# Hybrid encoder trunk: more seven-product tiles on the second feed-forward matrices, at other places

## The chip, the cores and the metric

The kernel runs on one core of a Trainium2 chip. The time is device microseconds of one launch. In the profile PE is TensorE (matmuls), PEld its weight loads, DVE the vector engine, ACT the scalar engine, SP the engine that issues most DMAs.

## The reference

Two layers on x of 256 tokens by 2048 features, everything in fp32: layer 0 is a 2-D neighbourhood attention (16 heads of 128), layer 1 a dilated windowed attention (three groups of eight heads). After each attention comes a feed-forward of width 8192, and at the end one more norm. What matters here is the feed-forward:

```python
def rms_norm(x, g):
    y = xf * lax.rsqrt(jnp.mean(xf * xf, axis=-1, keepdims=True) + EPS)
    return y * g

def sq_relu_mlp(h, w1, w2):
    return jnp.square(jax.nn.relu(h @ w1)) @ w2
...
for i in range(DEPTH):
    ...
    x = x + sq_relu_mlp(rms_norm(x, g), w1, w2)      # w1: 2048 x 8192, w2: 8192 x 2048
return rms_norm(x, final_norm)
```

Each feed-forward streams two matrices of 64 MB once through the core.

## The kernel before

**Products.** All of x stays in SBUF. Every fp32 operand is cut into a high and a low part in the matmul's format (`wh` and `wl` for weights): ACT rounds the high part, DVE subtracts it to get the low part. A product is three matmuls of 512 columns, high-high, high-low and low-high (`three`, lines 197 to 201).

**Steps.** The work is a list of 400 steps, issued in order. While step i's matmuls run in four quarters, `prep` cuts the weights of step i + 2 (lines 147 to 187), `load` fetches those of step i + 5, and small tasks (transposes, softmax pieces, norms) are hung into quarters. Every engine works through its own instructions in that order. Three buffers hold raw weights, four each hold halves of `wh` and `wl`.

**Calls, tiles and places.** In the feed-forwards the steps come in calls of `gemm_pair`, eight steps each. A call multiplies all 256 tokens by 1024 columns of a matrix, over a depth of 2048. One step is one **tile**, 256 deep, numbered 0 to 7 by its depth; its **place** (also 0 to 7) is when in the call it runs. A tile is a 2 by 2 by 2 block product, and is done in one of two ways:

- kind `"s"`: eight block products, 24 matmuls. `prep` makes two halves of `wh` and `wl`.
- kind `"x"`: seven block products (Winograd's form of Strassen's scheme), 21 matmuls. `prep_x` also adds blocks of the weights on DVE (`sums`, three instructions, and the block of `w` that is replaced), ACT rounds three sums (`hs`) and DVE makes their low parts (`ls`). The left operand needs sums too: `sums_and_parts` takes four 128-column blocks and makes the sums S1 to S3 and the parts, S1 standing in place of the block A21. With `keep` it leaves A21 and makes S1 as a fourth sum, so that the tile can be used either way.

The seven-product tiles of a call share four more PSUM banks ("1", "5", "6", "7"). In the place after the last of them `begin` combines these banks into the SBUF tile `C`. The last step's banks are added to `C` (`last_sum`) or the result goes to x (`early` adds `C` to x, `put` adds the call's other four banks).

**Groups.** A feed-forward (`ffn`) has four groups g of 2048 hidden features. A group has four calls: two on the first matrix (`cp` 0 and 1), each giving 1024 hidden features, then two on the second matrix over the depth of these 2048. After a call on the first matrix, `hidden` has ACT apply scale, relu and square to `C` (two instructions a quarter, during place 0 of the next call), PE transposes them at place 1, and four tiles of `hT` are made: a plain tile by one copy and one subtraction; a seven-product one by a copy to `raw` and, some places later, `parts_of`, which calls `sums_and_parts`.

In an eight-place order below, s and x are the kinds at places 0 to 7.

| call | tiles of kind x | order |
|---|---|---|
| first matrix, first call, g = 0 | 2, 4, 6 | ssxsxsxs |
| first matrix, first call, g > 0 | 2, 5, 4, 6 | ssxxsxxs |
| first matrix, second call | 2, 4, 6 | ssxsxsxs |
| second matrix, both calls, g < 3 | 2, 3, 5 | ssxsxsxs |
| second matrix, first call, g = 3 | 3, 5 | sssxsxss |
| second matrix, second call, g = 3 | 3, 5 | ssssxxss, in the second feed-forward ssxsxsss |

Tile 5 of the norm's output is the kept one: eight products in some calls, seven in others. A group's `early` additions to x, 1024 columns and twice 512, hang in the call that follows. In the last call of a feed-forward the last two steps are parted (`split_end`), so that half of the result is ready earlier.

Of the kernel before, what the change touches and what calls it, by code (L numbers as in the profile page):

```python
# [14 lines left out]
P = 128  # L15
T = 256
# [32 lines left out]
def tile_encoder(ctx: ExitStack, tc: tile.TileContext, ins, out):  # L49
# [324 lines left out]
    class Norm:  # L374
# [60 lines left out]
        def rstd(self):  # L435
            self.root()
            self.inverse()
            r = self.r
            self.rw = small.tile([P, 2, P], F32, name="rw", tag="rw", bufs=1)
            nc.vector.tensor_copy(self.rw, r.unsqueeze(2).to_broadcast([P, 2, P]))  # L440
# [7 lines left out]
        def rows_out(self):  # L448
            self.bc = small.tile([P, T], F32, name="rbc", tag="rbc", bufs=1)
# [19 lines left out]

    def sums_and_parts(b, t, half, sums):  # L470

        hi, lo = (t[:, 2 * half:2 * half + 2, h, :].rearrange("p a (u t) -> p a u t", u=2) for h in range(2))
        whole = b[:, 3:7, :].rearrange("p (a u) t -> p a u t", u=2)
        keep = sums.shape[2] == 4

        def own():
            nc.scalar.copy(hi, whole)
            subtract(nc.vector, lo, whole, hi.bitcast(F32))

        if keep:  # L480
# [6 lines left out]
        for n, src in ((slice(0, 3), b[:, 0:3, :]), (slice(3, 4), b[:, 4:5, :]))[:1 + keep]:  # L487
# [3 lines left out]
        for n, src in ((slice(0, 3), b[:, 0:3, :]), (slice(3, 4), b[:, 4:5, :]))[:1 + keep]:  # L491
            subtract(nc.vector, sums[:, 1, n], src, sums[:, 0, n].bitcast(F32))
# [47 lines left out]
    def pending_norm(get, bc):  # L540

        def chunk_done(step, c, delay=0, late=0):
            i = steps.index(step)
            for half in range(2):
                at(i + 1 + delay, lambda half=half: get().transposes(c, half), lambda half=half: get().parts(c, half),
                   quarter=1 + half + late)
            if c == NB - 1:
                if not bc:
                    at(i + 4, None, lambda: get().root())
                    at(i + 5, None, lambda: get().inverse())  # L550
                else:
                    at(i, None, lambda: get().rstd())
                    at(i + 2, lambda: get().rows(), lambda: get().rows_out())
                if get().perm:
                    at(i + 3, lambda: get().cols(), lambda: get().cols_out())
        return chunk_done
# [143 lines left out]

    FF_PAIRS, FF_KEPT = (2, 4, 6), (5,)
# [5 lines left out]
    out_rows(ins["na_wo"], na_oT, 4, lambda: norms[1], begin_norm(1, False, FF_PAIRS, FF_KEPT),  # L707
             [(c, k) for c in range(3) for k in range(3)] + [(c, 3) for c in range(3)] + [(3, k) for k in range(4)], 2)


    def ffn(norm, w1, w2, next_norm, next_done):
        for g in range(4):
            last = g == 3
            pairs2 = (3, 5) if last else (2, 3, 5)
            hT, sums = [None] * 4, {}

            def hidden(made, q, cp, hT=hT, sums=sums, pairs2=pairs2, last=last):
                i = steps.index(made[-1]) + 1
# [13 lines left out]
                for r in range(4):  # L732
# [10 lines left out]
                    def post(r=r, held=held):  # L743
                        c, half, pair = 2 * cp + r // 2, r % 2, 4 * cp + r
                        if half == 0:
                            hT[c] = opool.tile([P, 4, 2, T], F32R, name="hT", tag="o")
                        if pair in pairs2:
                            raw = blocks()
                            nc.scalar.copy(raw[:, 3:7, :].rearrange("p (a u) t -> p a (u t)", u=2), held["t"])

                            def parts_of(c=c, half=half, raw=raw, pair=pair):
                                sums[pair] = part.pool.tile([P, 2, 3, P], F32R, name="hs", tag="hsum", bufs=3)
                                sums_and_parts(raw, hT[c], half, sums[pair])
                            steps[i + (3 if cp else 2 * r - 1)].after[1].append(parts_of)
                        else:
                            to = hT[c][:, 2 * half:2 * half + 2]
                            split(to[:, :, 0, :], to[:, :, 1, :], held["t"])
# [3 lines left out]
            for cp in range(2):  # L761
                more = g and not cp
                order = ff_order(FF_PAIRS + FF_KEPT, (0, 1, 2, 5, 3, 4, 6, 7)) if more else ff_order(FF_PAIRS)
                gemm_pair(w1, 2 * g + cp, norm.xT, norm.sums, order, lambda made, q, cp=cp: hidden(made, q, cp))
# [6 lines left out]
            def residual(made, q, cp, parted, last=last):  # L771
# [12 lines left out]
                if not parted:  # L784
                    i = steps.index(made[-1])
                    for n in range(2):
                        if last:
                            made[-1].after[n].append(lambda n=n: early(n))
                        else:
                            at_after(i + (4 + 2 * n, 3 + 3 * n)[cp], 1, lambda n=n: early(n))  # L790
                    for m, (tb, c) in enumerate(QUARTERS):
# [23 lines left out]
            for cp in range(2):  # L815
                parted = last and cp == 1
                order = range(8) if last else (0, 1, 2, 4, 3, 6, 5, 7)
                if parted:
                    order = ((0, 1, 2, 4, 3, 5, 6, 7), (0, 1, 3, 2, 5, 4, 6, 7))[next_done is None]
                gemm_pair(w2g, cp, hT, sums, ff_order(pairs2, order), lambda made, q, cp=cp, parted=parted: residual(made, q, cp, parted),  # L820
                          parted, parted and next_done is not None)

# [133 lines left out]
    for hh in range(2):  # L956
# [16 lines left out]
        for h in range(4):  # L973
# [4 lines left out]
    parts[len(steps) + 2] = "feed-forward"  # L978
    out_rows(ins["dil_wo"], dil_oT, 2, lambda: norms[3], begin_norm(3, False, FF_PAIRS, FF_KEPT),
             [(0, 0), (1, 0), (0, 1), (1, 1), (2, 0), (2, 1), (3, 0), (3, 1)])  # L980
# [106 lines left out]
    for c in range(NB):  # L1087
        steps[(0, 1, 2, 2)[c]].post.append(lambda c=c: n0.squares(c))
    steps[2].post.append(n0.rstd)
# [102 lines left out]
```

## Time and profile before

| | us |
|---|---|
| median of 3 runs (2255.87 to 2257.86) | 2256.42 |
| the profiled execution | 2253.24 |
| its span, first to last instruction | 2251.5 |
| PE busy, DVE busy, ACT busy | 2238.7, 1891.8, 1269.2 |
| first feed-forward, from its first tile to its last call's first tile | 397.81 to 1035.90 |
| second feed-forward, the same | 1560.24 to 2199.14 |

A timeline row gives the start, the length, the engine, the source line, what is written from what, how many instructions were merged and, in brackets, the idle time before them with what ended it. A row of windows gives the busy time of each engine within a stretch. A matmul's record is longer than the time from one matmul to the next, since they are pipelined, and back-to-back DVE records overlap by less than 0.1 us. Counts such as x64 are of instructions in the stretch asked for.

### The profile page before, as it was taken

To read this page: it belongs to the slowest core of one execution; us is meant where nothing else is said; L and a number is where in the kernel's file an instruction comes from. 1 tells how busy PE (TensorE), PEld (TensorE's weight loads), DVE (VectorE), ACT (ScalarE), POOL (GpSimd) and SP (SyncE) were. 2 spreads that over 40 slices of the span, in tenths; PEclk is the share of its full clock that TensorE was granted. 3 is DMA by queue.
4 is the path that set the end of the run, shared out by engine and by line. 5 is a ranking of instruction groups with operands and counts; after the bars stand their busy time and mean duration, and the time that the engine had idled before them with its cause. 6 is when DMAs were issued, how large, how long until landed. Compare 5 with 4: busy or idle time off the path is not lost.

```text
span 2251.5 us, 28385 instructions
## 1 busy us (share of the span) xinstructions
PE 2238.7 (99%) x10906; PEld 1883.4 (84%) x10906; DVE 1891.8 (84%) x2217; ACT 1269.2 (56%) x1582; POOL 0.7 (0%) x6
## 2 busy tenths in 40 slices
PE   9999999999999999999999999999999999999998
PEld 8888888888888888888888888888888888888886
DVE  6776666899999999989877667757999999999988
ACT  6555455665665565565444544456665665665664
POOL 0000000000000000000000000000000000000000
PEclk9999999999999999999999999999999999999999
DMA  7556554656656666665555445444666666666664
GB/s 256 177 186 192 177 180 165 203 187 209 202 188 207 200 192 206 196 190 190 209 180 186 170 169 183 172 169 151 208 201 197 199 205 192 200 204 192 204 218 136
DMA packets 110728, 430.33 MB, mean 191 GB/s; under 512 B 23872, under 2 KB 24448, under 8 KB 92160
## 3 DMA queue, kind: packets, MB, share of 16 engines
q1 hardware_dynamic: 109920, 426.82, 58.1%
q8 instruction: 85, 1.39, 0.2%
q10 hardware_dynamic: 672, 1.70, 0.2%
q14 instruction: 51, 0.42, 0.1%
HBM read 426.38 MB, written 2.10 MB: 190 GB/s over the span
## 4 chain that ended last, share of the span: by engine, by line
PE 98%; DVE 1%; ACT 1%; issue 0%; ACTq 0%; POOLq 0%; POOL 0%; DVEq 0%
PE banks L199 25%; PE banks L201 25%; PE banks L200 25%; PE banks L229 13%; PE banks L234 7%; PE banks L740 1%; PE banks L393 1%; PE banks L940 0%; PE banks L900 0%; PE banks L635 0%; PE banks L1072 0%; PE banks L918 0%; PE banks L920 0%; ACT wh L194 0%; DVE wl L195 0%
## 5 line engine op out<-in xcount | busy, mean ns | idle before, releaser
L195 DVE TENSOR_TENSOR wl<-w,wh 128x1024 fp32r<-128x1024 f32 (+1 forms) x802 | 963.1, 1217 | 235.0 <-ACT wh L194 148.3
L194 ACT CAST wh<-w 128x1024 fp32r<-128x1024 f32 (+1 forms) x802 | 824.6, 1048 | 457.0 <-PE banks L201 306.3
L199 PE MATMUL banks<-wh,xT 128*128 128x512 f32 x1074 | 423.3, 394 | 0.0
L200 PE MATMUL banks<-wl,xT 128*128 128x512 f32 x1074 | 418.7, 390 | 0.0
L201 PE MATMUL banks<-wh,xT 128*128 128x512 f32 x1074 | 418.5, 390 | 0.0
L199 PE MATMUL banks<-wh,hT 128*128 128x512 f32 x804 | 316.2, 393 | 0.0
L201 PE MATMUL banks<-wh,hT 128*128 128x512 f32 x804 | 313.2, 390 | 0.0
L200 PE MATMUL banks<-wl,hT 128*128 128x512 f32 x804 | 312.9, 389 | 0.0
L229 PE MATMUL banks<-xT,wh 128*128 128x512 f32 x1280 | 312.5, 392 | 0.0
L229 PEld LDWEIGHTS banks<-xT,wh 128*128 128x128 f32 x1280 | 233.4, 188 | 44.2 <-ACT wh L194 0.2
L180 ACT CAST hs<-sums 128x1536 fp32r<-128x1536 f32 x98 | 145.3, 1482 | 186.5 <-DVE sums L138 186.5
L201 PEld LDWEIGHTS banks<-wh,xT 128*128 128x128 f32 x1074 | 201.6, 188 | 42.2
L200 PEld LDWEIGHTS banks<-wl,xT 128*128 128x128 f32 x1074 | 201.9, 188 | 40.6 <-DVE wl L195 1.2
L199 PEld LDWEIGHTS banks<-wh,xT 128*128 128x128 f32 x1074 | 201.9, 188 | 39.7
L201 PEld LDWEIGHTS banks<-wh,hT 128*128 128x128 f32 x804 | 150.9, 188 | 31.6
L200 PEld LDWEIGHTS banks<-wl,hT 128*128 128x128 f32 x804 | 151.1, 188 | 30.3
L135 DVE TENSOR_TENSOR ls<-sums,hs 128x1536 fp32r<-128x1536 f32 x98 | 171.6, 1751 | 5.6 <-ACT hs L180 5.6
L199 PEld LDWEIGHTS banks<-wh,hT 128*128 128x128 f32 x804 | 151.0, 188 | 30.0
L234 PE MATMUL banks<-xT,wl 128*128 128x256 f32 x1280 | 172.7, 284 | 0.1
L234 PEld LDWEIGHTS banks<-xT,wl 128*128 128x128 f32 x1280 | 165.8, 191 | 6.6 <-DVE wl L195 0.6
L138 DVE TENSOR_TENSOR sums<-w 128x1024 f32<-128x1024 f32 x98 | 119.4, 1218 | 0.0
L199 PE MATMUL banks<-wh,oT 128*128 128x512 f32 x192 | 76.6, 399 | 0.0
(186 smaller groups left out, 2348.7 us busy)
## 6 DMA issues: line engine op xcount, KB each, us to landing
w<-in_ffn_w_dram SPq DMA_DIRECT2D x512, 512.0 KB, 4.7
w<-in_dil_wqkv_dram SPq DMA_DIRECT2D x72, 1024.0 KB, 4.8
w<-in_na_wqkv_dram SPq DMA_DIRECT2D x47, 1024.0 KB, 5.2
w<-in_na_wo_dram SPq DMA_DIRECT2D x16, 1024.0 KB, 4.8
w<-in_dil_wo_dram SPq DMA_DIRECT2D x8, 1024.0 KB, 4.7
bias<-in_rpb_dram SPq DMA_DIRECT2D x32, 96.0 KB, 10.0
out_dram<-x SPq DMA_DIRECT2D x8, 256.0 KB, 2.6
x<-in_x_dram SPq DMA_DIRECT2D x3, 512.0 KB, 9.0
```

The source lines that it names most:

```text
L135: engine.tensor_tensor(out=out, in0=a, in1=b, op=ALU.subtract)
L138: engine.tensor_tensor(out=out, in0=a, in1=b, op=ALU.add)
L180: nc.scalar.copy(s.hs, s.sums)
L194: nc.scalar.copy(dst_hi, src)
L195: nc.vector.tensor_tensor(out=dst_lo, in0=src, in1=dst_hi.bitcast(F32), op=ALU.subtract)
L199: nc.tensor.matmul(o, left[0], right[0], start=start, stop=False)
L200: nc.tensor.matmul(o, left[0], right[1], start=False, stop=False)
L201: nc.tensor.matmul(o, left[1], right[0], start=False, stop=stop)
L229: nc.tensor.matmul(acc[j // 2][:, j % 2, :], s.hi[a][:, j * P:(j + 1) * P], xT[k][:, a].rearrange("p h t -> p (h t)"), start=k == 0 and a ...
L234: nc.tensor.matmul(acc[j // 2][:, j % 2, :T], s.lo[a][:, j * P:(j + 1) * P], xT[k][:, a, 0, :], start=False, stop=k == nk - 1 and a == 3)
L393: nc.tensor.transpose(self.tp[:, a, tb * P:(tb + 1) * P], x[:, tb, kt * P:(kt + 1) * P], ident)
L740: nc.tensor.transpose(t[:, a, tb * P:(tb + 1) * P], q["C"][:, 2 * tb + f // 4, f % 4 * P:(f % 4 + 1) * P], ident)
```

## The change

The second matrices' tile 6 becomes a seven-product tile in the second call of groups 0 to 2. In the first call it still is an eight-product one, so it is prepared with `keep`, but without the fourth sum: `first_sum` replaces A21 by S1 in place, at place 2 of the second call, from the difference of the parts. In the last group tile 2 joins tiles 3 and 5 in both calls. Orders and places change with it:

| call | tiles of kind x | order |
|---|---|---|
| first matrix, first call | unchanged, but the kept tile of the second feed-forward is 3 instead of 5 | as before |
| first matrix, second call | 2, 4, 6 | sssxsxxs |
| second matrix, first call, g < 3 | 2, 3, 5 | sssxsxxs |
| second matrix, second call, g < 3 | 2, 3, 5, 6 | ssxxsxxs |
| second matrix, both calls, g = 3 | 2, 3, 5 | ssxsxxss |

`parts_of` runs at place 2, and for tiles 3 and 6 at place 5 (before: at 3, and at 5 for tile 3). `early` hangs at places 2 and 5 after every call (before: 3 and 5 after a first call). In the last call of all, `begin` and `early` move one step later. Outside the feed-forward calls, `rstd`, `rows` and `cols` of the norm before the second attention come one step later, `rw` and `rbc` lie in the part's pool instead of the small one, and the squares of x's third quarter at the very start come within step 2 instead of after it.

```diff
-    def sums_and_parts(b, t, half, sums):
+    def sums_and_parts(b, t, half, sums, keep=False):
...
-        keep = sums.shape[2] == 4
+        kept = sums.shape[2] == 4
+        keep = keep or kept
...
-                    at(i, None, lambda: get().rstd())
-                    at(i + 2, lambda: get().rows(), lambda: get().rows_out())
+                    at(i + 1, None, lambda: get().rstd())
+                    at(i + 3, lambda: get().rows(), lambda: get().rows_out())
...
-            pairs2 = (3, 5) if last else (2, 3, 5)
+            pairs2, more = (2, 3, 5), () if last else (6,)
...
+                            def first_sum(t=hT[c], u=2 * half):
+                                d = blocks()
+                                subtract(nc.vector, d[:, 0:2, :], t[:, u, :, P:].bitcast(F32),
+                                         t[:, u + 1, :, P:].bitcast(F32))
+                                add(nc.vector, d[:, 2, :], d[:, 0, :], d[:, 1, :])
+                                nc.scalar.copy(t[:, u, 0, P:], d[:, 2, :])
+                                subtract(nc.vector, t[:, u, 1, P:], d[:, 2, :], t[:, u, 0, P:].bitcast(F32))
-                            steps[i + (3 if cp else 2 * r - 1)].after[1].append(parts_of)
+                            steps[i + (2, 5)[r == 3 or pair in more]].after[1].append(parts_of)
+                            if pair in more:
+                                steps[i + 10].after[1].append(first_sum)
...
-                more = g and not cp
-                order = ff_order(FF_PAIRS + FF_KEPT, (0, 1, 2, 5, 3, 4, 6, 7)) if more else ff_order(FF_PAIRS)
+                whole = [n for n in (0, 1, 3, 5, 7) if n not in norm.kept]
+                if cp:
+                    order = ff_order(FF_PAIRS, (0, 1, 3, 2, 5, 4, 6, 7))
+                elif g:
+                    order = ff_order(norm.pairs, (*whole[:2], 2, *norm.kept, whole[2], 4, 6, whole[3]))
+                else:
+                    order = ff_order(FF_PAIRS)
...
-                            at_after(i + (4 + 2 * n, 3 + 3 * n)[cp], 1, lambda n=n: early(n))
+                            at_after(i + 3 + 3 * n, 1, lambda n=n: early(n))
...
-                    (made[-3].evac if next_done is None else made[-2].after[1 + n]).append(lambda n=n: early(n))
+                    made[-2].after[1 + n].append(lambda n=n: early(n))
...
-                order = range(8) if last else (0, 1, 2, 4, 3, 6, 5, 7)
-                if parted:
-                    order = ((0, 1, 2, 4, 3, 5, 6, 7), (0, 1, 3, 2, 5, 4, 6, 7))[next_done is None]
+                if last:
+                    order = ff_order(pairs2, (0, 1, 2, 4, 3, 5, 6, 7))
+                elif cp:
+                    order = ff_order(pairs2 + more)
+                else:
+                    order = ff_order(pairs2, (0, 1, 4, 2, 7, 3, 5, 6))
```

More of the change, by code (lines that the diff above doesn't have):

```diff
@@ L438, in rstd @@
             r = self.r
-            self.rw = small.tile([P, 2, P], F32, name="rw", tag="rw", bufs=1)
+            self.rw = part.pool.tile([P, 2, P], F32, name="rw", tag="rw")
             nc.vector.tensor_copy(self.rw, r.unsqueeze(2).to_broadcast([P, 2, P]))
@@ L448, in rows_out @@
         def rows_out(self):
-            self.bc = small.tile([P, T], F32, name="rbc", tag="rbc", bufs=1)
+            self.bc = part.pool.tile([P, T], F32, name="rbc", tag="rbc")
             src, dst = self.bc_ps[:, 0, :], self.bc
@@ L486, in sums_and_parts @@
             nc.scalar.copy(hi, whole)
-        for n, src in ((slice(0, 3), b[:, 0:3, :]), (slice(3, 4), b[:, 4:5, :]))[:1 + keep]:
+        for n, src in ((slice(0, 3), b[:, 0:3, :]), (slice(3, 4), b[:, 4:5, :]))[:1 + kept]:
             nc.scalar.copy(sums[:, 0, n], src)
@@ L490, in sums_and_parts @@
             subtract(nc.vector, lo, whole, hi.bitcast(F32))
-        for n, src in ((slice(0, 3), b[:, 0:3, :]), (slice(3, 4), b[:, 4:5, :]))[:1 + keep]:
+        for n, src in ((slice(0, 3), b[:, 0:3, :]), (slice(3, 4), b[:, 4:5, :]))[:1 + kept]:
             subtract(nc.vector, sums[:, 1, n], src, sums[:, 0, n].bitcast(F32))
@@ L551, in chunk_done @@
                 else:
-                    at(i, None, lambda: get().rstd())
-                    at(i + 2, lambda: get().rows(), lambda: get().rows_out())
+                    at(i + 1, None, lambda: get().rstd())
+                    at(i + 3, lambda: get().rows(), lambda: get().rows_out())
                 if get().perm:
-                    at(i + 3, lambda: get().cols(), lambda: get().cols_out())
+                    at(i + 4, lambda: get().cols(), lambda: get().cols_out())
         return chunk_done
@@ L699, in begin_norm @@
         return pending_norm(lambda: norms[n], n == 2)
-    FF_PAIRS, FF_KEPT = (2, 4, 6), (5,)
+    FF_PAIRS = 2, 4, 6
     def ff_order(pairs, order=range(8)):
@@ L706, in tile_encoder @@
     parts = {len(steps) + 9: "feed-forward"}
-    out_rows(ins["na_wo"], na_oT, 4, lambda: norms[1], begin_norm(1, False, FF_PAIRS, FF_KEPT),
+    out_rows(ins["na_wo"], na_oT, 4, lambda: norms[1], begin_norm(1, False, FF_PAIRS, (5,)),
              [(c, k) for c in range(3) for k in range(3)] + [(c, 3) for c in range(3)] + [(3, k) for k in range(4)], 2)
@@ L713, in ffn, with hidden @@
             last = g == 3
-            pairs2 = (3, 5) if last else (2, 3, 5)
+            pairs2, more = (2, 3, 5), () if last else (6,)
             hT, sums = [None] * 4, {}
-            def hidden(made, q, cp, hT=hT, sums=sums, pairs2=pairs2, last=last):
+            def hidden(made, q, cp, hT=hT, sums=sums, pairs2=pairs2, more=more):
                 i = steps.index(made[-1]) + 1
@@ L746, in post @@
                             hT[c] = opool.tile([P, 4, 2, T], F32R, name="hT", tag="o")
-                        if pair in pairs2:
+                        if pair in pairs2 + more:
                             raw = blocks()
@@ L751, in parts_of @@
                             def parts_of(c=c, half=half, raw=raw, pair=pair):
-                                sums[pair] = part.pool.tile([P, 2, 3, P], F32R, name="hs", tag="hsum", bufs=3)
-                                sums_and_parts(raw, hT[c], half, sums[pair])
-                            steps[i + (3 if cp else 2 * r - 1)].after[1].append(parts_of)
+                                sums[pair] = part.pool.tile([P, 2, 3, P], F32R, name="hs", tag="hsum", bufs=4)
+                                sums_and_parts(raw, hT[c], half, sums[pair], pair in more)
+                            def first_sum(t=hT[c], u=2 * half):
[8 more added lines that the diff above has]
+                                steps[i + 10].after[1].append(first_sum)
                         else:
@@ L816, in ffn @@
                 parted = last and cp == 1
-                order = range(8) if last else (0, 1, 2, 4, 3, 6, 5, 7)
-                if parted:
-                    order = ((0, 1, 2, 4, 3, 5, 6, 7), (0, 1, 3, 2, 5, 4, 6, 7))[next_done is None]
-                gemm_pair(w2g, cp, hT, sums, ff_order(pairs2, order), lambda made, q, cp=cp, parted=parted: residual(made, q, cp, parted),
-                          parted, parted and next_done is not None)
+                if last:
[4 more added lines that the diff above has]
+                    order = ff_order(pairs2, (0, 1, 4, 2, 7, 3, 5, 6))
+                gemm_pair(w2g, cp, hT, sums, order, lambda made, q, cp=cp, parted=parted: residual(made, q, cp, parted),
+                          parted, parted)
     ffn(norms[1], ins["ffn0_w1"], ins["ffn0_w2"], lambda: norms[2], begin_norm(2, True))
@@ L978, in tile_encoder @@
     parts[len(steps) + 2] = "feed-forward"
-    out_rows(ins["dil_wo"], dil_oT, 2, lambda: norms[3], begin_norm(3, False, FF_PAIRS, FF_KEPT),
+    out_rows(ins["dil_wo"], dil_oT, 2, lambda: norms[3], begin_norm(3, False, FF_PAIRS, (3,)),
              [(0, 0), (1, 0), (0, 1), (1, 1), (2, 0), (2, 1), (3, 0), (3, 1)])
@@ L1087, in tile_encoder @@
     for c in range(NB):
-        steps[(0, 1, 2, 2)[c]].post.append(lambda c=c: n0.squares(c))
+        (steps[c].post if c < 2 else steps[2].after[0] if c == 2 else steps[2].post).append(lambda c=c: n0.squares(c))
     steps[2].post.append(n0.rstd)
```

## The prediction

> **What bounds the kernel now.** I read the page first, then the busy times of single calls, then the timeline of the vector engine beside TensorE's.
>
> ```profile
> span 2251.5 us, 28385 instructions
> PE 2238.7 (99%) x10906; PEld 1883.4 (84%) x10906; DVE 1891.8 (84%) x2217; ACT 1269.2 (56%) x1582; POOL 0.7 (0%) x6
> ...
> DVE  6776666899999999989877667757999999999988
> ...
> PE 98%; DVE 1%; ACT 1%; issue 0%; ACTq 0%; POOLq 0%; POOL 0%; DVEq 0%
> ```
>
> TensorE sets the end: the chain of waits is 98% PE. But the average of 84% for DVE hides two stretches of 9s, and these are the two feed-forwards. So I took one group of the first feed-forward (its second, g = 1) call by call: first matrices first call, second call, second matrices first call, second call. The fifth row is the last group's first call on second matrices.
>
> ```profile
> core 0: us, PE busy (x) PEld busy (x) DVE busy (x) ACT busy (x) POOL busy (x), PEclk, DMA share, GB/s
> 568.45:609.42 40.97, 40.97 (x181) 33.63 (x180) 40.56 (x41) 22.34 (x21) 0.00 (x0) 1.00 0.58 184
> 609.42:653.06 43.64, 43.64 (x201) 35.85 (x199) 42.09 (x49) 29.60 (x36) 0.00 (x0) 1.00 0.63 202
> 653.06:696.42 43.36, 43.36 (x201) 35.94 (x199) 40.58 (x45) 28.69 (x34) 0.00 (x0) 1.00 0.62 201
> 696.42:737.90 41.48, 41.48 (x185) 34.36 (x183) 38.43 (x39) 21.49 (x20) 0.00 (x0) 1.00 0.65 208
> 991.86:1035.90 44.04, 44.04 (x203) 36.49 (x202) 37.86 (x42) 27.43 (x33) 0.00 (x0) 1.00 0.58 188
> ```
>
> The group takes 169.45 us and DVE is busy for 161.66 of it: 7.8 us are left. The first call, with four seven-product tiles, leaves DVE 0.41 us. How far ahead DVE is there I read as a **lead**: the start of a tile's first matmul on `wl` minus the end of the DVE instruction that made that `wl`. DVE rows first, then PE's.
>
> ```profile
> 558.26 3.86 DVE L195 TENSOR_TENSOR wl<-w,wh 128x1024 fp32r<-128x1024 f32 x3
> 563.62 1.23 DVE L195 TENSOR_TENSOR wl<-w,wh 128x1024 fp32r<-128x1024 f32 x1 [1.49 <-ACT wh L194]
> ...
> 597.65 1.22 DVE L195 TENSOR_TENSOR wl<-w,wh 128x1024 fp32r<-128x1024 f32 x1
> 598.78 1.75 DVE L135 TENSOR_TENSOR ls<-sums,hs 128x1536 fp32r<-128x1536 f32 x1
> ...
> 602.79 4.62 DVE L195 TENSOR_TENSOR wl<-w,wh 128x1024 fp32r<-128x1024 f32 x4
> ```
>
> ```profile
> 568.68 0.39 PE L200 MATMUL banks<-wl,xT 128*128 128x512 f32 x1
> ...
> 599.28 0.39 PE L200 MATMUL banks<-wl,xT 128*128 128x512 f32 x1
> ...
> 600.64 0.45 PE L200 MATMUL banks<-ls,xs 128*128 128x512 f32 x1
> ...
> 604.12 0.44 PE L200 MATMUL banks<-wl,xT 128*128 128x512 f32 x1
> ```
>
> At the call's first tile the lead is 568.68 - 562.12 = 6.56 us, at place 6 599.28 - 598.87 = 0.41 (and 0.11 for `ls`), at the last tile 604.12 - 604.01 = 0.11. 600.64 minus 599.28 is six matmuls: 0.227 us each, so 21 make a seven-product tile of 4.76 us and 24 an eight-product tile of 5.44. The list of waits says that PE already waits at these two spots, once in each of the six four-tile calls:
>
> ```profile
> PEld banks L199 <- DVE hT L195: 2.6, 8, 0.4
> PEld banks L200 <- DVE ls L135: 1.3, 6, 0.2
> PEld banks L200 <- DVE wl L195: 1.2, 6, 0.2
> ```
>
> So TensorE is the bound by a margin that one four-tile call uses up, and it starts that call with all the lead there is.
>
> **The change, part by part.** Each feed-forward gets five more seven-product tiles: one in the second call of groups 0 to 2 and one in each call of the last group. Ten tiles save 10 x 3 x 0.227 = **6.8 us** of TensorE. What DVE pays:
>
> ```profile
> 578.60 1.22 DVE L138 TENSOR_TENSOR sums<-w 128x1024 f32<-128x1024 f32 x1
> ...
> 585.13 1.22 DVE L138 TENSOR_TENSOR x<-x,C 128x1024 f32<-128x1024 f32 x1
> ```
>
> ```profile
> 675.22 1.07 DVE L135 TENSOR_TENSOR h<-h 128x256 f32<-128x256 f32 x3
> 676.38 0.69 DVE L135 TENSOR_TENSOR hT<-h,hT 128x512 fp32r<-128x512 f32 x1
> 676.99 0.55 DVE L135 TENSOR_TENSOR hs<-h,hs 128x384 fp32r<-128x384 f32 x1
> 677.82 2.36 DVE L195 TENSOR_TENSOR wl<-w,wh 128x1024 fp32r<-128x1024 f32 x2 [0.29 <-ACT wh L194]
> ```
>
> - A seven-product tile's preparation runs from 578.60 to 585.13, 6.53 us; two `wl` of 1.14 (4.62 - 1.22 over three) are needed anyhow, so the extra is 4.26.
> - The sums of a hidden tile run from 675.22 to 677.82, 2.60 us with their waits for ACT, against about 0.60 for the plain split: 2.0 more. Tile 6 takes the `keep` order, where the 0.55 of `hs` begins only when ACT has rounded it; `wl` is queued behind that and ACT's `wh` too. I take 3.2, between 2.6 (this row) and 3.8 (1.05 more, a whole `wh`).
> - `first_sum` is not in the trace. Its three DVE pieces are like the `h` rows, 1.0 together; between them DVE waits for one ACT copy of 128 columns (between 0 and the 0.63 that a row below shows for 512; I take 0.35), and after them for ACT's `wh` of 1.03, queued behind that copy, up to 0.75. Between 1.3 and 2.1; I take 2.1, since ACT can start neither early there.
>
> By busy time alone (4.19 + 1.55 + 1.0) this is 6.7 us for each of groups 0 to 2. An inner group would have 7.8 - 0.7 = 7.1 us for it, if DVE never waited. It does wait, and the new places make it wait more: in first matrices' second call and second matrices' first call place 2 now is an eight-product tile, and ACT squares four quarters around its two `wh`. The trace has that pattern in the fifth call above:
>
> ```profile
> 993.02 0.73 ACT L722 ACTIVATE C<-C,rstd 128x512 f32<-128x512 f32 x1
> ...
> 999.09 1.03 ACT L194 CAST wh<-w 128x1024 fp32r<-128x1024 f32 x1
> ```
>
> ```profile
> 996.66 1.23 DVE L195 TENSOR_TENSOR wl<-w,wh 128x1024 fp32r<-128x1024 f32 x1 [1.05 <-ACT wh L194]
> 1000.16 1.22 DVE L195 TENSOR_TENSOR wl<-w,wh 128x1024 fp32r<-128x1024 f32 x1 [2.28 <-ACT wh L194]
> ...
> 1004.49 1.21 DVE L195 TENSOR_TENSOR wl<-w,wh 128x1024 fp32r<-128x1024 f32 x1
> ```
>
> ```profile
> 1010.29 0.39 PE L200 MATMUL banks<-wl,hT 128*128 128x512 f32 x1
> ```
>
> DVE stands idle for 3.3 us, and the seven-product tile at place 3 has a lead of 1010.29 - 1005.70 = 4.6. When DVE itself is late, ACT's squares start later too; I take 4.3.
>
> Now the **running balance** of the lead: add PE's time of a tile, take off DVE's work up to the next tile's first `wl`; under zero PE stalls (at a seven-product tile 0.3 earlier, for `ls`).
>
> - Four-tile call as today: 6.56 down to 0.11, of which 1.49 is DVE's idle time at 563.62. It needs 5.0 us of lead. The last tile then gives back 5.44 - 2 x 1.14, so the next call starts with 3.2.
> - Second matrices' second call (new): the same and `first_sum`, 7.1 needed. With 3.2 it stalls 3.9.
> - The next group's first call follows it with 3.2 where it had 6.6: stall 1.8.
> - First matrices' second call: 4.3 at place 3; up to place 4 DVE has `ls` 1.67 (1.75 less the 0.08 by which records overlap, as 1.22 and 1.14 for `wl`), two `wl`, one split and one tile's sums, 7.15 against 4.76: 1.9; to place 5 two `wl` and three additions of 2.59 together (6.53 - 1.67 - 2.27), 4.87 against 5.44: 2.5; to place 6 both that and `ls`, 6.54 against 4.76: 0.7; to place 7 `ls`, two `wl` and the sums, 6.55 against 4.76: stall 1.1.
> - Second matrices' first call: the same with 3.2 for 2.6 at the end: stall 1.7.
>
> An inner group: 3.9 + 1.8 + 1.1 + 1.7 = 8.5, less the 0.2 + 0.3 that it stalls today (the `ls`/`wl` and `hT` rows; the latter goes, since place 2 no longer opens new banks) = 8.0, less 0.7 for PE: **+7.3**. Group 0 has a three-tile first call, so its second call begins with full lead: 0.8 + 1.7 + 3.9 - 0.7 = +5.7. The last group: 1.8 + 1.1, and about 2.1 in its second matrices' first call, where tiles at places 4 and 5 come right after the sums at place 2; its last call begins with full lead and stalls nothing; less 0.5 and 1.4: +3.1. One feed-forward 5.7 + 2 x 7.3 + 3.1 = 23.4, two **+46.8**.
>
> The rest is small. In the last call of all, the combinations and early additions move from the third last tile into the second last.
>
> ```profile
> 2231.37 1.23 DVE L138 TENSOR_TENSOR x<-x,C 128x1024 f32<-128x1024 f32 x1
> ...
> 2234.86 0.68 DVE L138 TENSOR_TENSOR x<-x,banks 128x512 f32<-128x512 f32 x1
> ...
> 2238.78 0.69 DVE L138 TENSOR_TENSOR x<-x,banks 128x512 f32<-128x512 f32 x1 [0.28 <-PE banks L201]
> ```
>
> ```profile
> 2241.07 0.39 PE L201 MATMUL banks<-wh,hT 128*128 128x512 f32 x1
> ```
>
> PE's last two tiles are 48 matmuls and begin at 2230.4. Combinations (2.6) and additions (2.4) now start one quarter of a tile later, about 2232.5, instead of ending at 2233.8; with the two `x<-x,banks` and 1.6 us of gains and sums that follow, DVE reaches the work of 2238.78 some 1.3 us late, and from there the end is one dependent chain: +1.3 (bounds 0 and 2). The norm's `rstd`, row and column broadcasts come one step later, where the attention's first steps give DVE room (7s in its row); uncovered they are under 1 us. The kept tile of the second feed-forward's norm moves from 5 to 3, the same work earlier: 0, bounds -0.8 and +0.5. Squares in step 2, and `rw` and `rbc` in another pool: 0. SP issues as many loads as before, in another order; a load waits for DVE to free its buffer, but is needed only two tiles or more later, some 9.5 us against the 4.7 to landing below; uncovered, a late load would cost what is missing of 4.7.
>
> ```profile
> w<-in_ffn_w_dram SPq DMA_DIRECT2D x512, 512.0 KB, 4.7
> ```
>
>
> Sum: 46.8 + 1.3 = +48 on the profiled execution's 2253.24 us, 2301. The median of the runs shown is 2256.42, 3.2 higher, so I predict **2304**.
>
> **The rivals.**
>
> 1. *Lean DVE.* ACT's waits vanish because DVE comes late to them, and the bounds below hold (`first_sum` 1.3, tile 6 at 2.6). The lead at place 3 of the two middle calls is then about 6 instead of 4.3, so they end at 6 - 5.4 = 0.6 without a stall; the inner group's last call starts with 3.8 and needs 6.3, stall 2.5, the next first call 1.8: 4.3 - 0.5 - 0.7 = +3.1. Group 0's last call has full lead: -0.7. Last group 1.8 + 1.1 - 0.5 - 1.4 = +1.0. Twice (6.2 - 0.7 + 1.0) and 1.3 give +14: 2271. The row at 1000.16 speaks against it.
> 2. *Faster.* DVE's idle time fills completely: it decides if the added work with its waits stays under 7.1 us in an inner group. Then nothing stalls and the 6.8 are gained: 2249.6. For it: 6.7 is under 7.1. Against it: the 3.3 at 996.66 and 1000.16, and that the two heavy calls are neighbours. The Trainium skill's Perfetto Trace Analysis (Engine Utilization) gives the vector engine's 100% as 245.76 G elements a second in fp32; by that an extra tile's 3584 columns are an estimated 1.9 us and this rival would hold. The trace disagrees: `ls` takes 1.75 us for 128x1536, which is 112 G a second.
> 3. *The two cancel.* Stalls between 2 and 11 us: 2252 to 2261. Nothing in the balance gives that; it needs half of rival 1's stalls away.
> 4. *A slower clock.* Today PEclk is 1.00 in every call above. If the second call's stalls made TensorE run the next tile at half speed, that tile costs 4.76 more, six times: +29, 2333. The Trainium skill's TensorE: Matmul & The Clock Gate (Part 1) puts the throttle after about 3.4 us of idle; the balance has no single stall that long (the largest is 2.1, at `first_sum`). No row here shows such a stall.
>
> **How the numbers follow.** My forecast 0.70, rival 1 0.15, rival 2 0.06, rival 3 0.05, rival 4 0.04. The forecast's own range is 2291 to 2320. Down: `first_sum` at 1.3 in six groups 5, tile 6 at 2.6 4, a lead of 4.6 at place 3 in 14 calls 4. Up: tile 6 at 3.8 4, and 12 if ACT's squares slip by 0.9 more in those 14 calls, with DVE's own lateness. Reaching to rival 1, the range is 2268 to 2320. A change under 0.2% (4.5 us) can't be told from none here. Faster 0.06, same 0.05, slower 0.89.
>
> **What would show it.** Right: in the waits, PEld behind DVE's `wl` and `ls` grows from 2.5 us to about 55; an inner group grows from 169.5 to about 177 with DVE busy near 168; the second call of second matrices is about 45 instead of 41.5; DVE shows idle before `wl` of 1 to 2 us at the start of two calls in each group. Wrong: PE's chain unbroken with call lengths of 40.8 there (rival 2); no idle time at those two places (rival 1); PEclk under 1.00 in the feed-forward (rival 4).

## The result: slower, 2306.6 us

| | before | after |
|---|---|---|
| median (6 runs each) | 2255.25 | 2306.60 (2305.22 to 2307.76) |
| ratio, 95% interval | | 1.0233, 1.0223 to 1.0244 |
| span | 2251.5 | 2305.9 |

The page of the changed kernel, the lines that answer to those of before:

```profile
span 2305.9 us, 28475 instructions
PE 2255.9 (98%) x10876; PEld 1879.0 (81%) x10876; DVE 1948.2 (84%) x2307; ACT 1284.8 (56%) x1614; POOL 0.7 (0%) x6
...
DVE  6767666899999999999877666758899999999998
...
PE 82%; DVE 11%; ACT 4%; issue 2%; DMA 0%; ACTq 0%; DVEq 0%; POOLq 0%; SPq 0%; POOL 0%
```

The chain of waits, 98% PE before, is 82% PE and 11% DVE now, though DVE's share of the span is still 84%. Single calls show it. The rows are the second call on the second matrix in group 0, the four calls of group 1 in the order of the prediction's first four rows, and the last group's first call on the second matrix.

```profile
core 0: us, PE busy (x) PEld busy (x) DVE busy (x) ACT busy (x) POOL busy (x), PEclk, DMA share, GB/s
530.65:575.26 44.61, 42.22 (x182) 33.41 (x180) 43.15 (x46) 22.31 (x22) 0.00 (x0) 1.00 0.60 188
575.26:617.85 42.59, 41.71 (x181) 33.43 (x180) 42.18 (x43) 22.10 (x21) 0.00 (x0) 1.00 0.62 198
617.85:662.29 44.44, 43.68 (x200) 35.86 (x199) 41.24 (x48) 29.69 (x36) 0.00 (x0) 1.00 0.59 189
662.29:707.53 45.24, 43.97 (x200) 35.86 (x199) 41.41 (x48) 29.55 (x36) 0.00 (x0) 1.00 0.58 186
707.53:752.16 44.63, 43.13 (x181) 34.75 (x180) 43.16 (x46) 22.33 (x22) 0.00 (x0) 0.96 0.59 189
1015.99:1060.92 44.93, 43.95 (x201) 35.77 (x199) 42.80 (x48) 28.68 (x34) 0.00 (x0) 1.00 0.60 197
```

The group takes 176.90 us instead of 169.45, with DVE busy for 167.99. PE's busy time is now shorter than the call in all of them. What its weight loads waited for, over the whole span:

```profile
engine line waited for: us in total, times, longest us
PEld banks L200 <- DVE wl L195: 39.2, 43, 1.4
PEld banks L199 <- ACT wh L194: 13.5, 18, 1.2
PEld banks L200 <- DVE ls L135: 9.4, 26, 0.4
PEld banks L199 <- DVE gx L421: 3.0, 1, 3.0
```

The waits for `hT` at place 2 are gone, as said, and 48.6 us behind DVE's low parts stand where 2.5 were (about 55 were said), with 13.5 behind `wh`, which the prediction had not listed. The last row was not foreseen either; it is taken up below.

### The profile page after: what moved, and what is told of

It reads as the page before. It is cut to its first block, busy times and chain, and to the rows that moved or that the text cites. A ratio compares the mean times of both kernels' runs of the same rounds, so it can differ in the third digit from the quotient of the medians.

```text
span 2305.9 us, 28475 instructions
## 1 busy us (share of the span) xinstructions
PE 2255.9 (98%) x10876; PEld 1879.0 (81%) x10876; DVE 1948.2 (84%) x2307; ACT 1284.8 (56%) x1614; POOL 0.7 (0%) x6
## 4 chain that ended last, share of the span: by engine, by line
PE 82%; DVE 11%; ACT 4%; issue 2%; DMA 0%; ACTq 0%; DVEq 0%; POOLq 0%; SPq 0%; POOL 0%
PE banks L200 20%; PE banks L201 20%; PE banks L199 20%; PE banks L229 13%; PE banks L234 7%; DVE wl L195 5%; ACT wh L194 3%; DVE sums L138 3%; PE banks L741 1%; DVE x L138 1%; DVE ls L135 1%; DVE w L138 1%; PE banks L393 1%; ACT hs L180 1%; DVE C L138 0%
## 5 line engine op out<-in xcount | busy, mean ns | idle before, releaser
L194 ACT CAST wh<-w 128x1024 fp32r<-128x1024 f32 (+1 forms) x802 | 816.2, 1046 | 349.9 <-PE banks L201 225.2
L180 ACT CAST hs<-sums 128x1536 fp32r<-128x1536 f32 x108 | 160.3, 1484 | 290.0 <-DVE sums L138 290.0
L200 PE MATMUL banks<-wl,hT 128*128 128x512 f32 x754 | 297.4, 394 | 14.6 <-DVE wl L195 14.6
L199 PE MATMUL banks<-wh,hT 128*128 128x512 f32 x754 | 300.0, 398 | 7.3 <-ACT wh L194 7.3
L201 PE MATMUL banks<-wh,hT 128*128 128x512 f32 x754 | 295.5, 392 | 0.0
L135 DVE TENSOR_TENSOR ls<-sums,hs 128x1536 fp32r<-128x1536 f32 x108 | 189.1, 1751 | 0.3 <-ACT hs L180 0.3
L200 PEld LDWEIGHTS banks<-wl,hT 128*128 128x128 f32 x754 | 142.7, 189 | 49.9 <-DVE wl L195 21.9
L199 PEld LDWEIGHTS banks<-wh,hT 128*128 128x128 f32 x754 | 142.3, 189 | 40.7 <-ACT wh L194 12.3
L201 PEld LDWEIGHTS banks<-wh,hT 128*128 128x128 f32 x754 | 142.5, 189 | 29.5
L138 DVE TENSOR_TENSOR sums<-w 128x1024 f32<-128x1024 f32 x108 | 131.5, 1217 | 0.0
L138 DVE TENSOR_TENSOR sums<-sums,w 128x512 f32<-128x512 f32 x108 | 74.8, 692 | 3.7
```

Of the source, the lines that this page charges most:

```text
L135: engine.tensor_tensor(out=out, in0=a, in1=b, op=ALU.subtract)
L138: engine.tensor_tensor(out=out, in0=a, in1=b, op=ALU.add)
L180: nc.scalar.copy(s.hs, s.sums)
L194: nc.scalar.copy(dst_hi, src)
L199: nc.tensor.matmul(o, left[0], right[0], start=start, stop=False)
L200: nc.tensor.matmul(o, left[0], right[1], start=False, stop=False)
```

## The experiments

The theory is the balance of the lead: DVE's own instructions, and the time in which ACT holds it up, are what comes late. Rivals to it stand in the expectations. In the first four runs the kernel before measured 2253.6, in the next four 2253.85, then 2253.35 and 2253.07; the changed kernel stands at 2306.6. All diffs but the last two are against the changed kernel; the last two are against the kernel before, but leave in place the changed kernel's edits outside the feed-forward calls.

**Places back.** The ten added tiles stay, but the two middle calls of a group get their old places.

```diff
-order = ff_order(FF_PAIRS, (0, 1, 3, 2, 5, 4, 6, 7))          # first matrix, second call
+order = ff_order(FF_PAIRS)
-order = ff_order(pairs2, (0, 1, 4, 2, 7, 3, 5, 6))            # second matrix, first call
+order = ff_order(pairs2, (0, 1, 2, 4, 3, 7, 5, 6))
-steps[i + (2, 5)[r == 3 or pair in more]].after[1]
+steps[i + (5 if pair in more else 3 if cp else 2 * r - 1)].after[1]
```

> The changed kernel with the same seven-product tiles, but in the two calls between (first matrices' second call, second matrices' first call) the old places 2, 4, 6 and the sums of hidden tiles at their old places (tile 6 at place 5). DVE's and TensorE's work is the same as in the changed kernel. Theory (the lead of DVE, with its waits for ACT at the new places, sets the stalls): the two calls between stall 0.3 and 0 us instead of 1.1 and 1.7, and the last group's first call on second matrices about 0.7 less; 9.3 us less in each feed-forward, so 2306.6 - 18.6 = 2288. Rival (the total of DVE's work alone sets it, the places don't matter): 2306, within 3.

Measured 2291.42, ratio 1.0166 (1.0150 to 1.0181): beside the added tiles, the new places cost 15.2 us. Busy times of the two middle calls of group 1:

```profile
613.95:657.59 43.64, 43.64 (x200) 35.86 (x199) 42.09 (x49) 29.61 (x36) 0.00 (x0) 1.00 0.63 198
657.59:701.12 43.53, 43.53 (x201) 35.86 (x199) 40.70 (x47) 29.40 (x36) 0.00 (x0) 1.00 0.59 190
```

They are 0.8 and 1.7 us shorter than in the changed kernel, and the four-tile calls stay at 42.56 and 44.65. The whole gain is 3.4 short of the 18.6 expected, in the main because the last group's first call on the second matrices still takes 44.75, and the first feed-forward's last call grows from 48.31 to 49.60.

**No tile 6 in the second calls** (so no `keep` and no `first_sum`; the new places and the last group's tiles stay).

```diff
-pairs2, more = (2, 3, 5), () if last else (6,)
+pairs2, more = (2, 3, 5), ()
-order = ff_order(pairs2 + more)
+order = ff_order(pairs2, (0, 1, 2, 4, 3, 6, 5, 7))
```

> The changed kernel without the seven-product tile 6 in the second calls of groups 0 to 2 (those calls as before the change, three tiles at 2, 4, 6; so no first_sum and no keep). Theory: the second call regains full length of 41.5 without a stall, the next first call starts with a lead near 6 and stalls 0.2; of the change the new places (1.1 in each of the calls between) and the last group stay: 2 us for each of six groups and 2 for each last group, and 7 outside these: about 2278. Rival (the loss sits in the places and the last group): above 2295. Rival (the tile in the second call is all of it): 2255.

Measured 2269.55, ratio 1.0068 (1.0053 to 1.0083): lower than expected. The second call on the second matrices, with three such tiles again, is back at 41.48, and the four-tile call after it at 40.97; second matrices' first call has 43.59, since without tile 6 there are no sums at its place 5, which the expectation had counted.

**The new places alone**, with the tiles of before.

```diff
-pairs2, more = (2, 3, 5), () if last else (6,)
+pairs2, more = (3, 5) if last else (2, 3, 5), ()
```

> Tiles as before the change in every call on second matrices (2, 3, 5; last group 3, 5), but the new places 3, 5, 6 in the two calls between and the sums of hidden tiles at 2 and 5. Theory (DVE waits for ACT's squares at place 0 and is late at place 7): each of these calls stalls 1.1 us in groups 0 to 2 and none in the last group, 12 us in all, and 1 to 4 more outside the calls: 2268 to 2271. Rival (places 3, 5, 6 help, because banks needed for the seven products are free by then, the 2.6 us of waits for hT go): 2250 to 2255.

Measured 2259.25, ratio 1.0025 (1.0016 to 1.0035). Slower, as the theory had it, but by 5.7 and not by 14: first matrices' second call, with sums at both places 2 and 5, pays 0.9, second matrices' first call, with sums at place 2 alone, 0.2.

```profile
610.12:654.61 44.49, 43.72 (x201) 35.85 (x199) 41.29 (x48) 29.67 (x36) 0.00 (x0) 1.00 0.60 189
654.61:698.17 43.56, 43.56 (x201) 35.85 (x199) 40.79 (x45) 28.66 (x34) 0.00 (x0) 1.00 0.62 193
```

These runs split the 53.0 us: 5.7 for the places (and the small edits, which all of them keep), 2269.55 - 2259.25 = 10.3 for the last group's tiles, 37.0 for tile 6 in six second calls. About half of the 10.3 is one call, the first feed-forward's last, 49.33 instead of 44.47. The places cost 5.7 beside the old tiles and 15.2 beside the new ones: the difference of 9.5 is paid for the two together.

**Early additions on GpSimd**, to take 2.4 us off DVE in each four-tile call.

```diff
+e = nc.vector if last else nc.gpsimd
-add(nc.vector, o, o, C[:, 0:2, :]...)
+add(e, o, o, C[:, 0:2, :]...)            # and the two of 512 columns likewise
```

> The changed kernel with the early additions to x (1024 columns and twice 512 after each call on second matrices, but for the last group's) on GpSimd instead of DVE. It takes 2.3 us of DVE's work out of each four-tile call that follows. Theory (DVE is the bound there): 2.3 less in the second call, 1.8 less in the next first call, 12.3 in each feed-forward: 2282, if GpSimd's additions end before DVE comes to the same rows of x and don't slow DVE down. Rival (TensorE waits for something else than DVE's throughput): 2306. If GpSimd's use slows DVE, its rows get longer and the time lies between.

Measured 2335.38, ratio 1.0361 (1.0346 to 1.0377): all its expectations fall, the last one too: DVE's rows do get longer, but the time does not lie between. GpSimd's rows, and DVE's beside them:

```profile
579.89 3.26 POOL L138 TENSOR_TENSOR x<-x,C 128x1024 f32<-128x1024 f32 x1 [39.25 <-issue]
583.12 2.27 POOL L135 TENSOR_TENSOR x<-x,C 128x512 f32<-128x512 f32 x1
```

```profile
580.81 3.42 DVE L138 TENSOR_TENSOR sums<-w 128x1024 f32<-128x1024 f32 x1
584.27 1.67 DVE L138 TENSOR_TENSOR sums<-sums,w 128x512 f32<-128x512 f32 x1
585.97 1.67 DVE L138 TENSOR_TENSOR w<-sums,w 128x512 f32<-128x512 f32 x1
```

While GpSimd adds, DVE's three additions for a tile take 6.76 us instead of 2.6 (1.22 and twice 0.69). So DVE loses 4.2 us to be rid of 2.4; the two calls grow to 44.40 and 47.56. This says nothing against the theory, but does not test it either. The Trainium skill's GPSIMD Engine Reference (Specifications) says that GpSimd's SBUF interfaces are shared with the vector engine, and that DVE instructions with two SBUF inputs contend; the trace agrees, with 3.42 for 1.22 us.

**No early additions** in groups 0 to 2: the clean form of that test.

```diff
 def early(n):
+    if not last:
+        return
```

> The changed kernel without the early additions of C to x in groups 0 to 2 (this leaves that part of the result out, nothing else). They are 1.22 + 2 x 0.69 = 2.6 us of DVE, 2.4 without the overlap of the records, and hang only in the two four-tile calls: second matrices' second call and the next group's first call. Balance of the lead (DVE's own work is what is late): the second call of second matrices goes from 44.63 to about 42.2, the next first call from 42.59 to about 41.0, since 3.2 of lead then covers the 2.6 that are needed. 6 x (2.4 + 1.6) = 24 us less: 2282 (2278 to 2288). Rival, ACT's roundings set the pace of these calls and DVE's additions only fill its waits: 2300 to 2307.

Measured 2288.15, ratio 1.0152 (1.0137 to 1.0167): 18.4 less, not 24. Second matrices' second call and the next group's first call:

```profile
704.12:747.52 43.40, 41.90 (x181) 33.49 (x180) 41.93 (x44) 22.32 (x22) 0.00 (x0) 1.00 0.60 194
747.52:788.33 40.81, 40.81 (x182) 33.79 (x181) 40.38 (x41) 22.27 (x21) 0.00 (x0) 1.00 0.64 212
```

The next first call loses its whole 1.8: 40.81 is 180 matmuls with no stall. The second call loses only 1.22, the first addition at place 2. The second pair hangs at place 5, and what it frees comes after the call's last stall, at place 6: at the last place the lead is 1.34 instead of 0.23, and the next call begins with 4.51 instead of 3.40. 6 x (1.22 + 1.79) = 18.1.

**No first_sum.**

```diff
-if pair in more:
-    steps[i + 10].after[1].append(first_sum)
```

> The changed kernel without first_sum (tile 6 then multiplies with A21 in the place of S1 in the second calls: that part of the result is wrong). It hangs in six calls that all stall, so whatever it costs DVE is seen in full. By the prediction's upper bound, 2.1 each: 12.6 less, 2294. By its lower bound, 1.3 each: 2299. Rival, it lies in time that DVE spends waiting in any case: 2305 to 2307. The call goes from 44.63 to 42.5, 43.3 or 44.5.

Measured 2294.28, ratio 1.0179 (1.0164 to 1.0195): 12.3 less, the upper bound of 2.1 a call. The call goes to 42.55. In the trace of the changed kernel, where it does run (DVE):

```profile
726.91 0.42 DVE L135 TENSOR_TENSOR h<-hT 128x256 f32<-128x256 f32 x1
727.37 0.29 DVE L138 TENSOR_TENSOR h<-h 128x128 f32<-128x128 f32 x1
728.02 0.29 DVE L135 TENSOR_TENSOR hT<-h,hT 128x128 fp32r<-128x128 f32 x1 [0.36 <-ACT hT L761]
728.97 2.36 DVE L195 TENSOR_TENSOR wl<-w,wh 128x1024 fp32r<-128x1024 f32 x2 [0.65 <-ACT wh L194]
```

One microsecond of arithmetic on 128 columns costs 728.97 - 726.91 = 2.06, half of it two trips to ACT.

**Without the squares**: ACT's work around the two `wh` of the middle calls, halved.

```diff
-nc.scalar.activation(c, c, AF.Square)          # in squared_relu
```

> The changed kernel without the second of ACT's two instructions for each quarter of hidden features (the square is left out, the features are relu alone). ACT then has 4 x 0.73 = 2.9 us less around its two wh in first matrices' second call and second matrices' first call. Theory of the prediction, these instructions hold up wh, DVE idles and the seven-product tile at place 3 has a lead of only 4.3: DVE's idle time falls, the lead rises to 5.5 or more, first matrices' second call goes from 44.45 to about 43.4 and second matrices' first call from 45.2 to about 43.8; 8 x 1.0 + 6 x 1.4 less: 2290 (2286 to 2296). Rival, the places of the sums of hidden tiles alone make these calls late: 2303 to 2307.

Measured 2289.42, ratio 1.0159 (1.0144 to 1.0174), as the theory had it. The two middle calls:

```profile
613.87:657.23 43.36, 43.36 (x201) 35.94 (x200) 41.78 (x48) 27.90 (x32) 0.00 (x0) 1.00 0.61 197
657.23:700.88 43.65, 43.65 (x201) 35.86 (x199) 41.00 (x48) 27.69 (x32) 0.00 (x0) 1.00 0.58 190
```

DVE's `wl` for place 3, first in the changed kernel, then without the squares:

```profile
626.27 1.23 DVE L195 TENSOR_TENSOR wl<-w,wh 128x1024 fp32r<-128x1024 f32 x1 [1.98 <-ACT wh L194]
```

```profile
620.63 1.23 DVE L195 TENSOR_TENSOR wl<-w,wh 128x1024 fp32r<-128x1024 f32 x1 [0.34 <-ACT wh L194]
```

DVE's idle time falls from 1.98 to 0.34, and the lead at place 3 rises from 4.5 to 6.1. So the new places lose because DVE waits for ACT there with an eight-product tile at place 2; the sums at place 5 then use up what lead is left: in the changed kernel's second call on first matrices it is 4.46, 2.07, 2.65 and 0.88 at places 3 to 6, with the stall at place 7, as the balance had it (4.3, 1.9, 2.5, 0.7).

**The last call in another order.** In the changed kernel, the first feed-forward's last call opens its four extra banks at place 2, and PE stands still:

```profile
1075.46 0.39 PE L201 MATMUL banks<-hs 128*128 128x512 f32 x1
1078.46 0.50 PE L199 MATMUL banks<-hs 128*128 128x512 f32 x1 [2.61 <-DVE gx L421]
```

From that call's start to the second feed-forward's start it is 528.92 us, 524.34 before: 4.6 more, where the prediction had 0.7 less. The call itself has 3.84 of it, 48.31 instead of 44.47; the rest comes much later and is no loss (see the run fewest). Here the seven-product tiles go to places 3, 4 and 5:

```diff
-order = ff_order(pairs2, (0, 1, 2, 4, 3, 5, 6, 7))
+order = ff_order(pairs2, (0, 1, 4, 2, 3, 5, 6, 7))      # in that one call
```

> The changed kernel with its seven-product tiles at places 3, 4 and 5 instead of 2, 4 and 5 in the first feed-forward's last call alone. In the changed kernel PE waits 2.61 us at place 2 of that call for the next norm's pieces (they hold the banks that the tile opens), and eight matmuls after it take 0.427 us instead of 0.227. If both are the cause of the unpredicted 4.6 us, the tile comes 5.4 us later, the banks are free, and both go: 2302.4 (2301.5 to 2303.5), with no slow matmuls at that place. Rival, DVE is behind by then anyway and the wait comes back as one for wl or ls: 2305 to 2307.

Measured 2307.57, ratio 1.0238 (1.0221 to 1.0255): the rival; the call takes 48.87. The waits of its weight loads from 1060 to 1100:

```profile
PEld banks L200 <- DVE wl L195: 4.6, 3, 1.8
PEld banks L200 <- DVE ls L135: 0.9, 2, 0.4
```

The wait for the banks is gone, and 5.5 us behind `wl` and `ls` stand in its place. The banks were where DVE's lateness showed, not its cause: in this call DVE also makes the next norm's pieces, eight `gx` of 0.48 and eight subtractions of 0.43. In the kernel before it was busy for 40.57 of that call's first 42.70 us, so that 2.1 were left for a tile that costs 4.3.

**Fewer tiles**, from the kernel before: only where its trace shows lead.

```diff
-pairs2 = (3, 5) if last else (2, 3, 5)
+pairs2 = (2, 3, 5)     # last group: first call ssxsxsxs, early additions in quarters 2 and 3;
+                       # last call of all ssxxxsss; the first feed-forward's last call keeps 3 and 5
+# second feed-forward's norm keeps tile 3 instead of 5
```

> The old orders and places everywhere, no tile 6 in second calls, and a seventh-product tile added only where the trace of before shows lead to spare: tile 2 in the last group's first call on the second matrix, at the order ssxsxsxs, where the other groups run 43.36 instead of 44.04 (the early additions there go to quarters 2 and 3 of its last step); tile 2 also in the last call of all, at places 2, 3 and 4, so that combinations and additions stay where they are today; the first feed-forward's last call keeps two (tile 2 gets the fourth sum). The second feed-forward keeps tile 3 instead of 5, as in the changed kernel, where its first tile then took 6.37 instead of 7.13. Balance of the lead: no new stall in the first calls, each 0.68 less; the last call 0.68 less if DVE keeps up with three such tiles in a row, no gain if not; 0.76 for the kept tile. -2.1 to -2.8 on the kernel before, 2250.8 to 2251.5 where that is at 2253.6, a ratio of 0.9988 to 0.9991. Rival, tiles at these places are paid by DVE here too: 2254 to 2258, ratio 1.000 to 1.002.

Measured 2257.61, ratio 1.0019 (1.0009 to 1.0028): the rival. The tile in the first call does pay, and the last call takes back more. The second feed-forward's calls:

```profile
2155.90:2199.26 43.36, 43.36 (x201) 35.93 (x199) 41.75 (x46) 28.70 (x34) 0.00 (x0) 1.00 0.69 230
2199.26:2243.00 43.74, 40.45 (x172) 31.55 (x171) 42.35 (x48) 21.93 (x29) 0.00 (x0) 1.00 0.33 106
```

43.36 instead of 44.04 is the 0.68; three seven-product tiles in a row leave PE busy for 40.45 of 43.74 us, and the last call takes 56.74 instead of 52.32. In the first feed-forward the tile saves 0.68 too, but the last call, with the two tiles of before, takes 45.66 instead of 44.47: its first transposes for the norm wait for the early additions, which come later. By a slip, tile 2 got its fourth sum in every group of the first feed-forward, not only in the last; its second calls on the first matrix grew by 0.1 to 0.4 us for it.

**The two pieces that seemed left**: the kept tile 3, and tile 2 in the second feed-forward's last group, first call only.

```diff
-pairs2 = (3, 5) if last else (2, 3, 5)
+pairs2 = (3, 5) if last and next_done is not None else (2, 3, 5)   # last call of all: (3, 5) as before
```

> The kernel before with only the two pieces left that a call of its trace can pay: tile 3 kept instead of 5 for the second feed-forward (0.76 off its first tile), and there, in the last group's first call on the second matrix, tile 2 as a third seven-product tile at the order ssxsxsxs (43.36 instead of 44.04, 0.68 off), with the fourth sum so that the last call of all stays as it was. The first feed-forward's calls and orders are those of before. Of the changed kernel's other edits, rw and rbc in the part's pool, rstd, rows and cols a step later and the squares of the third quarter stay. -1.4 us: 2252.0 where the kernel before is at 2253.4, ratio 0.9994. Rival, the later rstd, rows and cols cost the attention after it 1 us (524.34 to 526.30 from the first feed-forward's last call to the second's first in the run fewer): ratio 0.9998 to 1.0000.

Measured 2253.82, ratio 1.0004 (0.9995 to 1.0013): no difference that can be told. The windows are the second feed-forward's first call (43.17 before) and the call with the added tile:

```profile
1560.19:1602.62 42.43, 42.43 (x193) 35.13 (x192) 38.45 (x48) 26.59 (x32) 0.00 (x0) 1.00 0.67 213
...
2154.36:2197.72 43.36, 43.36 (x200) 35.93 (x199) 42.42 (x47) 28.79 (x34) 0.00 (x0) 1.00 0.70 232
```

Both calls are shorter, by 0.74 and 0.68, but the last call goes from 52.32 to 53.91: its first seven-product tile, which had a lead of 0.7 before, now waits for `wl`. And the 0.74 is no gain. From the first feed-forward's last call to the second's first tile it is 525.10 instead of 524.34, 0.76 more, and that is the same wait at another spot: PE's transposes of x wait for an addition to x that DVE makes behind the kept tile's sums. In the kernel before, they do so in the second feed-forward's first tile:

```profile
1563.17 0.33 PE L393 MATMUL banks<-ident,x 128*128 128x128 f32 x1
1563.77 0.55 PE L393 MATMUL banks<-ident,x 128*128 128x128 f32 x3 [0.27 <-DVE x L516]
```

With tile 3 kept instead of 5, those sums come earlier, and so does the wait (in this run; the changed kernel has it 9.0 us before the second feed-forward's start too):

```profile
1550.63 0.30 PE L393 MATMUL banks<-ident,x 128*128 128x128 f32 x1
1551.13 0.55 PE L393 MATMUL banks<-ident,x 128*128 128x128 f32 x3 [0.21 <-DVE x L517]
```

So the rival's 0.76 is there, but the later `rstd`, rows and columns are not its place.

## Why the prediction was right, and where not

Forecast 2304, measured 2306.6, inside its own range of 2291 to 2320; rivals 1 to 3 fall, with the stalls in the trace.

- **The balance held call by call.** Second matrices' second call 44.63 - 40.81 = 3.8 of stall (3.9 said), the next first call 1.8 (1.8), first matrices' second call 44.44 - 43.36 = 1.1 (1.1), second matrices' first call 1.9 (1.7); inner group +7.5 (+7.3), group 0 +5.9 (+5.7), the last group's first three calls +3.2 (+3.8). From a feed-forward's first tile to its last call's first tile it is 24.1 and 23.2 more, 24.0 in the second without the 0.76 of the moved wait. The prediction's 23.4 had 0.7 off for the last call, so 24.1 up to there. That this is met to 0.1 is partly luck, as the last group's miss cancels those of the others.
- **The prices held.** `first_sum` 2.06 (2.1), the lead at place 3 4.4 to 4.5 (4.3), shown by the runs without first_sum and without the squares. Tile 6's sums, from the trace of the changed kernel, take 700.86 - 697.54 = 3.32 (3.2):

```profile
697.54 0.68 DVE L135 TENSOR_TENSOR hT<-h,hT 128x512 fp32r<-128x512 f32 x1
...
699.92 0.56 DVE L135 TENSOR_TENSOR hs<-h,hs 128x384 fp32r<-128x384 f32 x1 [0.58 <-ACT hs L489]
700.86 4.63 DVE L195 TENSOR_TENSOR wl<-w,wh 128x1024 fp32r<-128x1024 f32 x4 [0.39 <-ACT wh L194]
```

- **"Its last call begins with full lead and stalls nothing" failed** for the first feed-forward: +3.84 instead of -0.7. Most of the lead was there at the call's start, 5.05 where it was 5.88 before; the step left out the norm's pieces that DVE makes in the call.
- **The tail** was undersized: the last call of all takes 53.94 instead of 52.32, +1.6, where -0.7 and +1.3 make +0.6. To its last matmul's start the call gains 0.3 instead of 0.7, since its weight loads wait 0.8 us for DVE where they waited for nothing before; behind that matmul 1.9 are lost instead of 1.3, within the bounds of 0 and 2. No run tried why.
- **The kept tile** was taken as 0, and that is what it is worth: the second feed-forward's first tile goes from 7.13 to 6.37, and a wait of the same 0.7 to 0.8 comes 9 us before it instead. Up to the first feed-forward the kernel is 0.9 later (398.74 instead of 397.81), which the prediction had at 0; the other ten runs, with the same instructions up to there, lie at 397.05 to 398.88, so it is not the edits' doing for sure.
- **Luck in the number.** 4.5 for the first feed-forward's last call, 1.0 for the tail and 0.9 for the start make the 6.4 that the profiled execution's 54.4 has over the 48 forecast. The medians differ by less, 51.35, and the 48 were added to 2256.42, the highest median that the kernel before has on record. So the 2304 came out 2.6 from 2306.6, closer than the sum of its terms.
- **Rival 4 had its mechanism right and its price wrong.** The clock did drop, three times, without a stall as long as it asked for, and where six drops were priced at 29 us these cost under 1 us together (below).

## What to carry to other kernels

When one engine is the bound by a few microseconds a stage, a busy share of 84% elsewhere says little: follow how far ahead the feeding engine is at each point where its result is needed, and add up its queue, its waits included. An operation that saves 0.68 us on the bound and costs 4.3 on its feeder pays only where the lead to spend is neither needed by the next stage nor already given away; of the two places here that seemed to have some, one only moved a wait, and the other, worth 0.68 us, made a later call longer by more than that. A wait in the trace names where lateness shows, and an order that avoids it only moves it unless the late engine has less to do. A call that got shorter is a gain only if the stretch before it did not get longer.

## What the runs showed of the hardware

**The clock drops after short stalls, and the slow stretch mostly fills time in which PE would have waited.** In the changed kernel's fifth window above PEclk is 0.96. PE around `first_sum` there:

```profile
727.86 0.39 PE L201 MATMUL banks<-hs,hT 128*128 128x512 f32 x1
728.99 0.50 PE L199 MATMUL banks<-wh,hT 128*128 128x512 f32 x1 [0.74 <-ACT wh L194]
730.25 0.50 PE L200 MATMUL banks<-wl,hT 128*128 128x512 f32 x1 [0.76 <-DVE wl L195]
...
731.27 0.63 PE L200 MATMUL banks<-wl,hT 128*128 128x512 f32 x1
731.70 0.63 PE L201 MATMUL banks<-wh,hT 128*128 128x512 f32 x1
```

Two stalls of 0.74 and 0.76 us, and then matmuls 0.43 apart instead of 0.227. The same happens after the 2.61 at 1078.46. Granted clock in both stretches:

```profile
730.00:734.00 4.00, 3.75 (x10) 2.95 (x11) 3.93 (x6) 1.61 (x2) 0.00 (x0) 0.60 0.52 130
1079.00:1083.00 4.00, 4.00 (x12) 3.10 (x11) 3.90 (x7) 0.00 (x0) 0.00 (x0) 0.58 0.49 165
```

Each slow stretch lasts about 3.2 us, and adds some 1.6. Yet the call with it takes 44.63 and group 0's, at a clock of 1.00, 44.61: DVE sets the end, so PE's slow matmuls only fill what would have been the next stall. Group 2's call, with the second such stretch, takes 44.75. Behind the bank wait it did cost something: the run no_early has the same last call and the same wait, but no slow stretch, and takes 47.72 there instead of 48.31. The Trainium skill's TensorE: Matmul & The Clock Gate (Part 1) has the half rate come after an idle window of about 3.4 us, which is free-running; the stretch's length fits one window, but the stalls here were shorter than one, the two of 0.74 and 0.76 far shorter. Why the same two stalls drop the clock in groups 1 and 2 of the first feed-forward and in no other group, the runs don't show. It is not their place in the program: in the run last_order, the same up to there, they do not drop it in those two groups, but do in the second feed-forward's group 2.

**GpSimd beside DVE** is dear: 3.26 us for an addition of 128x1024 that takes DVE 1.22, while it stretches DVE's own from 1.22 to 3.42.
